# Where the activation tiles lie in SBUF: each at another multiple of 64 bytes past a 512-byte boundary, the weight tiles on the boundary as before

## The chip, the cores and the metric

One Trainium2 chip, one of its cores. The metric is the device time of one execution in microseconds (us); the kernel is run several times and the median is compared. All tensors are float32; most matmuls read their operands as float32r (`F32R` in the code).

## The reference, cut to what matters

One layer of a hybrid encoder on 256 tokens with a model width of 2048: an input projection to attention and to a gated recurrence (HGRN2), both mixed and projected, a squared-ReLU MLP of width 8192, a per-layer embedding with a gate, and a final RMSNorm. Nearly all of its arithmetic is in the products of the 256 x 2048 activations with weight matrices:

```python
proj = jnp.einsum('bsd,de->bse', rmsnorm(x, g_mix[i]), w_in[i])
...
y_attn = jnp.einsum('bse,ed->bsd', bidirectional_gqa(q_a, k_a, v_a), w_o_attn[i])
y_hgrn = jnp.einsum('bse,ed->bsd', o_r, w_o_hgrn[i])
mixed = jax.nn.sigmoid(gate_a) * y_attn + jax.nn.sigmoid(gate_r) * y_hgrn
x = x + jnp.einsum('bsd,de->bse', mixed, w_out[i])
u = jnp.square(jax.nn.relu(jnp.einsum('bsd,df->bsf', rmsnorm(x, g_mlp[i]), w_up[i])))
x = x + jnp.einsum('bsf,fd->bsd', u, w_down[i])
ple_gate = jax.nn.sigmoid(jnp.einsum('bsd,de->bse', rmsnorm(x, g_ple[i]), w_ple_gate[i]))
x = x + ple_gate * jnp.einsum('bsc,cd->bsd', p[i].astype(x.dtype), w_ple[i])
return rmsnorm(x, g_final)
```

## The kernel before

Every operand of a large product is split in two float32r parts, `hi` (a rounded copy) and `lo` (the rest), and three of the four partial products are summed: hi x hi, hi x lo and lo x hi.

Weights stream from HBM one 1 MB tile at a time, in the order of a list made beforehand (`order`, `plan`). `load` brings a tile into `raw` (three buffers), `prep_half` lets ScalarE copy half of it to a `hi` tile (L112) and VectorE subtract to get the `lo` tile (L113). `hi` and `lo` have four buffers of 4096 bytes per partition each.

Activations stand in tiles of 16384 bytes per partition, shaped [128, 8, 2, 256]: eight blocks of 128 features, for each the hi and the lo part, for each 256 tokens. Two such tiles make the 2048 features. They come from `bigt`, which takes the next of six buffers of one pool (`big`), and in two later stages from pools on the right-hand side of SBUF (`MX0`, `MX1`; `UB0`, `UB1`). `bigt` also gives the buffers of x, the residual rows and the final gain.

There are two forms of product:

- `gemm_mov` (L196): the stationary operand, which TensorE loads ahead of a matmul, is a 128x128 piece of an activation tile; the moving operand, which streams through, is 512 columns of a weight tile. All projections but two stages use it, w_ple's product (L699) has the same form. 5,232 matmuls in all.
- `gemm_st` (L177 and L178): the stationary operand is a piece of a weight tile; the moving operand is a block of an activation tile. L177 streams hi and lo of the activations together (512 columns) past the hi weights, L178 streams hi alone (256 columns) past the lo weights, and the two alternate. 1,792 such pairs: 768 in the recurrence's inputs (between some 229 and 713 us), 1,024 in the MLP's up-projection.

The recurrence (`scan_head`) and attention (`attend`) are generators, and small pieces of their work are put between the large matmuls; their tiles (`QQ`, `KK`, `kc`, `SD` and others; `qT`, `kT`, `pt`, `va`) come from right-hand pools too. PE runs its instructions in the order of the program; every matmul has a weight load of its own, which is issued when the matmul ahead of it starts.

A tile's byte address within a partition follows from the order and sizes of the pools. A tile without further use (`pad`, or the unnamed `ctile([P, 104])`) moves what stands behind it. What the address leaves when it is divided by 512 is called the offset here. In the kernel before, these are the offsets of what TensorE reads:

| Tiles | read at | offset before |
|---|---|---|
| weights `hi`, `lo` | L177, L178, L196 | 0 |
| activations `big`, `MX`, `UB` | L177, L178, L196 | 0 |
| `kT` moving, `qT` stationary | L424 | 352, 224 |
| `pt` moving, `va` stationary | L444 | 224, 224 |
| `QQ`, `kc`, `KK`, `SD` | L510, L536, L544 | 448 |

Pieces inside such tiles start at whole multiples of 512 bytes, so these are the offsets of every read.

Of the kernel before, what the change touches and what calls it, by code (L numbers as in the profile page):

```python
# [4 lines left out]
F32 = mybir.dt.float32  # L5
# [7 lines left out]
P = 128  # L13
# [13 lines left out]
def build(tc, xT, xtok, pT, gains, gfin_in, ropet, ident_in, masks_in, ghg_in, lb_in,  # L27
# [4 lines left out]
    def view(t, off, dims):  # L32
        return bass.AP(t.tensor, t.offset + off, [list(t.ap[0])] + [list(d) for d in dims])
# [35 lines left out]
    with contextlib.ExitStack() as es:  # L69
        def open_pool(name, bufs=1, **kw):  # L70
            st = contextlib.ExitStack()
            p = st.enter_context(tc.tile_pool(name=name, bufs=bufs, **kw))
            return p, st
# [4 lines left out]
        big, st_ = open_pool("big", 6); es.enter_context(st_)  # L78
# [5 lines left out]
        def nm(s):  # L84
            cnt[0] += 1
            return f"{s}_{cnt[0]}"

        def bigt(dt, shape):
            return big.tile(shape, dt, tag="big", name=nm("big"))

        def gps():
            return psg.tile([P, 512], F32, tag="g", name=nm("g"))
# [46 lines left out]
        def weave(gen):  # L139
            woven.append([gen, 0.0])  # L140
# [14 lines left out]
        def flush():  # L155
            while woven:
                advance(min(woven, key=lambda en: en[1]))
# [8 lines left out]
        def xs(X, k):  # L166
            return X[k // 8][:, k % 8]

        def gemm_st(key, X, last=None):

            his, los = next_w(key)
            ps = gps()
            for k in range(KT):
                if k == 12 and last:
                    last()
                x = xs(X, k)
                pe.matmul(ps, wsl(his, k, P), x, start=k == 0, stop=False)  # L177
                pe.matmul(ps[:, :S], wsl(los, k, P), x[:, 0, :], start=False, stop=k == KT - 1)  # L178
                tick(0.327)
            return ps  # L180

        def merge(ps, z):
            act.activation(z, ps[:, S:], AF.Copy)
            dve.tensor_tensor(z, ps[:, :S], z, ALU.add)
            return z

        def gemm_mov(arr, j, X, last=None, stagger=False):

            ps = [gps() for _ in range(NT)]

            def chunk(c, w, ts):
                for a, ws in ((0, w[0]), (1, w[0]), (0, w[1])):
                    for kk in range(4):
                        k = 4 * c + kk
                        for t in ts:
                            last_mm[0] = pe.matmul(ps[t], xs(X, k)[:, a, t * P:(t + 1) * P], wsl(ws, kk, 512),  # L196
                                                   start=k == 0 and a == 0 and ws is w[0],
                                                   stop=k == KT - 1 and ws is w[1])
                        tick(0.216 * len(ts))

            for c in range(2 if stagger else 4):
                if c == 3 and last:
                    last()
                chunk(c, next_w((arr, j, c)), range(NT))
            if stagger:
                if last:
                    last()
                ws = [next_w((arr, j, c)) for c in (2, 3)]
                for t in range(NT):
                    for c in (2, 3):  # L210
                        chunk(c, ws[c - 2], (t,))
            return ps

        def proj(g, X):
            return gemm_mov("in", GROUPS.index(g), X)

        def to_T(srcs, X, e0, gain=None):

            yield 2.5
            for e in (e0, e0 + 2):  # L220
                tp = mps()
                for a in range(2):
                    for t in range(NT):
                        o = (e - e0 + a) * P
                        pe.transpose(tp[:, a * S + t * P:a * S + (t + 1) * P], srcs[t][:, o:o + P], ident)  # L225
                if gain is None:
                    dst = X[e // 8][:, e % 8:e % 8 + 2]
                    tv = tp.rearrange("p (e t) -> p e t", e=2)
                    act.activation(dst[:, :, 0, :], tv, AF.Copy)
                    dve.tensor_tensor(dst[:, :, 1, :], tv, dst[:, :, 0, :], ALU.subtract)  # L230
                else:
                    for a in range(2):
                        dst, tv, g = xs(X, e + a), tp[:, a * S:(a + 1) * S], gain[:, e + a:e + a + 1]
                        act.activation(dst[:, 0, :], tv, AF.Copy, scale=g)
                        dve.scalar_tensor_tensor(dst[:, 1, :], tv, g, dst[:, 0, :], ALU.mult, ALU.subtract)  # L235
                yield 0.5
# [18 lines left out]
        rp = t1([P, 2, 2 * NT, HD], "qT")  # L255
        mkf = t1([P, len(LEVELS), P], "pt")
        xf = bigt(F32, [P, KT, S])
        xg = bigt(F32, [P, KT, S])
        Hx = [bigt(F32R, [P, 8, 2, S]) for _ in range(2)]
        Hm = []  # L260
        quarter = lambda X, qd: X[qd // 2][:, 4 * (qd % 2):4 * (qd % 2) + 4]
# [332 lines left out]
        for j in range(4):  # L594
            ya, yb = ctok("ya"), ctok("yb")
            ps = proj(f"a{j}", Hm)
            for t in range(NT):
                act.activation(ya[t], ps[t], AF.Sigmoid)
            ps = gemm_mov("oa", j, OA)
            for t in range(NT):  # L600
                dve.tensor_tensor(ya[t], ps[t], ya[t], ALU.mult)
            ps = proj(f"b{j}", Hm)
            for t in range(NT):
                act.activation(yb[t], ps[t], AF.Sigmoid)
            if j == 0:
                flush()
                st2.close()
                ph3, st3 = open_pool("ph3", side="right")
                MX = [ph3.tile([P, 8, 2, S], F32R, tag=f"MX{i}", name=nm("MX")) for i in range(2)]
                ph3.tile([P, 120], F32, tag="pad", name=nm("pad"))  # L610
            ps = gemm_mov("oh", j, OH)
            for t in range(NT):
                dve.tensor_tensor(yb[t], ps[t], yb[t], ALU.mult)
                dve.tensor_tensor(ya[t], ya[t], yb[t], ALU.add)
            weave(to_T(ya, MX, 4 * j))
# [10 lines left out]
        def squares(i, j, t):  # L626
            act.activation(junk(), rows(j)[t], AF.Square, accum_out=sums[i][:, t, j:j + 1])

        def row_r(i, ts=slice(0, NT)):

            r = rr[i][:, ts]
            dve.tensor_reduce(r, sums[i][:, ts], AX.X, ALU.add)
            dve.tensor_scalar(r, r, 1.0 / D, EPS, ALU.mult, ALU.add)  # L633
            rsq(r, r, ts.stop - ts.start)
# [12 lines left out]
        for step in MLP:  # L647
            c = int(step[1])
            if step[0] == "u":
                for f in range(16):  # L650
                    ps = gemm_st(("up", c * 16 + f), H1, last=flush if c == f == 0 else None)
                    if c == f == 0:
                        st3.close()
                        ph4, st4 = open_pool("ph4", side="right")

                        def t4(shape, tag, bufs=2, dt=F32):
                            return ph4.tile(shape, dt, tag=tag, bufs=bufs, name=nm(tag))

                        row_r(0)
                        dve.tensor_tensor(r1s, rr[0], rr[0], ALU.mult)  # L660
                        UA = [bigt(F32R, [P, 8, 2, S]) for _ in range(2)]
                        UB = [t4([P, 8, 2, S], f"UB{i}", 1, F32R) for i in range(2)]
                        t4([P, 120], "pad", 1)
                    r = merge(ps, t4([P, S], "r"))
                    uu = t4([P, S], "uu")
                    dve.scalar_tensor_tensor(uu, r, 0.0, r, ALU.max, ALU.mult)
                    u = xs(UA if c % 2 == 0 else UB, f)
                    act.activation(u[:, 0, :], uu, AF.Copy)
                    dve.tensor_tensor(u[:, 1, :], uu, u[:, 0, :], ALU.subtract)
                continue  # L670
            if c == 3:
                Hp = [bigt(F32R, [P, 8, 2, S]) for _ in range(2)]
            for j in range(4):
                ps = gemm_mov("dn", 4 * c + j, UA if c % 2 == 0 else UB)
                for t in range(NT):
                    xj = rows(j)[t]
                    dve.scalar_tensor_tensor(xj, ps[t], r1s[:, t:t + 1], xj, ALU.mult, ALU.add)
                    if c == 3:
                        squares(1, j, t)
                if c == 3:  # L680
                    weave(to_T(rows(j), Hp, 4 * j, gn[:, 2]))
# [137 lines left out]
```

## Time and profile before

| | |
|---|---|
| median of 3 runs | 1988.33 us (1988.01 to 1990.47) |
| profiled execution, its own time | 1988.49 us |
| its span, first to last instruction | 1986.7 us |
| mean granted TensorE clock | 0.997 of full speed |
| PE busy | 1960.8 us, 99% of the span |
| DVE, ACT busy | 62%, 48% |
| mean DMA rate | 180 GB/s |

The span is what the trace covers; the execution's own time is 1.8 us longer. PE is TensorE's matmuls, PEld its weight loads, DVE is VectorE, ACT is ScalarE. A matmul's end is modelled in this profile: it stands some 160 ns after the start of the next one, so the pace of a stream is read from starts, and the "mean ns of one" of two matmul groups differ by as much as their paces do.

### The profile page before, as it was taken

Reading aid. Unit: us, or ns where it says so; the run is one execution under the profiler, and the core shown is the slowest. Engines: PE = TensorE matmul, PEld = TensorE weight load, DVE = VectorE, ACT = ScalarE, POOL = GpSimd, SP = SyncE. Lnnn points to the kernel's source line nnn. Section 1 sums busy time; section 2 is a strip of 40 time slices with the busy share of each in tenths; the row PEclk is TensorE's granted clock in tenths of the full one; section 3 lists DMA queues with packets and bytes.
Section 4 is the critical chain, followed back from the end, with each engine's and each line's share of the span. In section 5 each row is a group of like instructions: output and inputs, shape, how many; then the busy total and the mean of one; then the engine's idle time right before and its main releaser. Section 6 shows DMA issues by size and latency. Waiting matters only on the chain.

```text
span 1986.7 us, 25647 instructions
## 1 busy us (share of the span) xinstructions
PE 1960.8 (99%) x9948; PEld 1661.6 (84%) x9948; DVE 1237.5 (62%) x1722; ACT 947.6 (48%) x1495; POOL 144.9 (7%) x175
## 2 busy tenths in 40 slices
PE   8999999999999999999999999999999999999998
PEld 6788888888888888888888888888888888888886
DVE  6877687686785884445545566665565456545555
ACT  5576555454554554434434454443344344434543
POOL 3300030120220210000000000000000000000001
PEclk9999999999999999999999999999999999999999
DMA  8444444544434445555565555555555555555553
GB/s 324 168 146 149 149 149 148 173 146 162 165 140 170 159 141 189 190 191 191 190 234 196 191 173 188 191 190 192 191 188 191 194 185 181 199 196 177 208 194 123
DMA packets 51673, 358.56 MB, mean 180 GB/s; under 512 B 5984, under 2 KB 6240, under 8 KB 9056
## 3 DMA queue, kind: packets, MB, share of 16 engines
q1 hardware_dynamic: 51552, 356.93, 50.7%
q8 instruction: 78, 1.28, 0.2%
q14 instruction: 43, 0.35, 0.0%
HBM read 354.81 MB, written 2.10 MB: 180 GB/s over the span
## 4 chain that ended last, share of the span: by engine, by line
PE 96%; DVE 2%; issue 1%; ACT 1%; DMA 0%; SPq 0%; POOLq 0%; POOL 0%; DVEq 0%; ACTq 0%
PE g L196 58%; PE g L177 20%; PE g L178 10%; PE m L510 3%; DVE lo L113 1%; PE m L444 1%; PE m L424 1%; PE g L699 1%; PE m L225 1%; PE m L545 0%; PE m L530 0%; PE m L544 0%; PE m L455 0%; ACT hi L112 0%; PE m L396 0%
## 5 line engine op out<-in xcount | busy, mean ns | idle before, releaser
L113 DVE TENSOR_TENSOR lo<-raw,hi 128x1024 fp32r<-128x1024 f32 x660 | 811.7, 1248 | 645.2 <-ACT hi L112 589.5
L112 ACT ACTIVATE hi<-raw 128x1024 fp32r<-128x1024 f32 x660 | 679.0, 1055 | 801.1 <-PE g L196 457.7
L196 PE MATMUL g<-hi,big 128*128 128x512 f32 x2688 | 657.8, 393 | 9.6 <-ACT hi L112 9.6
L177 PE MATMUL g<-big,hi 128*128 128x512 f32 x1792 | 645.4, 403 | 0.0
L196 PEld LDWEIGHTS g<-hi,big 128*128 128x128 f32 x2688 | 500.8, 189 | 111.5 <-ACT hi L112 10.7
L178 PE MATMUL g<-big,lo 128*128 128x256 f32 x1792 | 502.6, 281 | 0.0
L177 PEld LDWEIGHTS g<-big,hi 128*128 128x128 f32 x1792 | 337.2, 188 | 78.6 <-DVE big L235 0.2
L196 PE MATMUL g<-lo,big 128*128 128x512 f32 x1344 | 343.8, 393 | 0.0
L178 PEld LDWEIGHTS g<-big,lo 128*128 128x128 f32 x1792 | 339.2, 189 | 0.4
L196 PEld LDWEIGHTS g<-lo,big 128*128 128x128 f32 x1344 | 249.1, 188 | 49.3 <-DVE lo L113 0.2
L196 PE MATMUL g<-hi,UB 128*128 128x512 f32 x512 | 122.1, 390 | 0.0
L196 PEld LDWEIGHTS g<-hi,UB 128*128 128x128 f32 x512 | 95.8, 188 | 19.7
L301 POOL TENSOR_TENSOR c<-c,c 128x2 f32<-128x2 f32 (+1 forms) x5 | 3.2, 640 | 1159.9 <-DVE c L633 1145.8
L510 PE MATMUL m<-QQ,kc 128*128 128x128 f32 x448 | 72.7, 285 | 3.1 <-ACT kc L502 2.7
L510 PEld LDWEIGHTS m<-QQ,kc 128*128 128x128 f32 x448 | 63.8, 190 | 11.6 <-ACT kc L502 5.6
L502 ACT ACTIVATE kc<-KK 128x256 f32<-128x256 f32 x112 | 47.8, 437 | 50.9 <-PE m L510 26.0
L524 POOL TENSOR_TENSOR T<-T 128x256 f32<-128x256 f32 (+2 forms) x96 | 54.0, 563 | 202.3 <-DVE T L588 186.5
L196 PE MATMUL g<-lo,UB 128*128 128x512 f32 x256 | 64.1, 391 | 0.0
L196 PE MATMUL g<-hi,MX 128*128 128x512 f32 x256 | 61.7, 391 | 0.0
L517 DVE TENSOR_TENSOR QQ<-QQ,T 128x256 f32<-128x256 f32 x112 | 52.1, 465 | 12.8 <-PE m L510 12.3
L514 DVE TENSOR_TENSOR KK<-KK,T 128x256 f32<-128x256 f32 x112 | 54.7, 491 | 5.5 <-ACT kc L502 2.6
L196 PEld LDWEIGHTS g<-lo,UB 128*128 128x128 f32 x256 | 47.8, 188 | 9.8
(145 smaller groups left out, 1099.3 us busy)
## 6 DMA issues: line engine op xcount, KB each, us to landing
raw<-w_mov SPq DMA_DIRECT2D x87, 1024.0 KB, 4.8
raw<-w_up SPq DMA_DIRECT2D x64, 1024.0 KB, 4.8
raw<-w_dn SPq DMA_DIRECT2D x64, 1024.0 KB, 4.8
raw<-w_st SPq DMA_DIRECT2D x48, 1024.0 KB, 4.8
raw<-w_oa SPq DMA_DIRECT2D x16, 1024.0 KB, 4.8
raw<-w_oh SPq DMA_DIRECT2D x16, 1024.0 KB, 4.8
raw<-w_out SPq DMA_DIRECT2D x16, 1024.0 KB, 4.8
raw<-w_pg SPq DMA_DIRECT2D x16, 1024.0 KB, 4.8
```

Source lines behind the costliest of these rows:

```text
L112: act.activation(hi, sl, AF.Copy)
L113: dve.tensor_tensor(lo, sl, hi, ALU.subtract)
L177: pe.matmul(ps, wsl(his, k, P), x, start=k == 0, stop=False)
L178: pe.matmul(ps[:, :S], wsl(los, k, P), x[:, 0, :], start=False, stop=k == KT - 1)
L196: last_mm[0] = pe.matmul(ps[t], xs(X, k)[:, a, t * P:(t + 1) * P], wsl(ws, kk, 512), start=k == 0 and a == 0 and ws is w[0], stop=k == KT ...
L225: pe.transpose(tp[:, a * S + t * P:a * S + (t + 1) * P], srcs[t][:, o:o + P], ident)
L424: pe.matmul(sc[:, t * S:(t + 1) * S], qT[:, i, a, t * P:(t + 1) * P], kT[:, j, b], start=n == 0, stop=n == 2)
L502: act.activation(kc.rearrange("p (n a b) -> p n a b", a=2, b=L), merged(KK, 0, L, S // (2 * L)), AF.Copy)
L510: pe.matmul(pl[:, t * P:(t + 1) * P], kc[:, t * P:(t + 1) * P], merged(QQ, t * P, L, P // (2 * L)), start=True, stop=True)
L514: dve.tensor_tensor(kv, kv, view(T, 1, [[2, nb // 2], [nb - 1, 2], [0, L]]), ALU.mult)
L517: dve.tensor_tensor(qv, qv, view(T, nb + 1, [[2, nb // 2], [-(nb + 1), 2], [0, L]]), ALU.mult)
L524: pool.tensor_tensor(Tn, view(T, 0, [[nb, 2], [2, nb // 2]]), view(T, 1, [[nb, 2], [2, nb // 2]]), ALU.mult)
```

## The change

`bigt` now takes 4096 + 16 elements (16448 bytes) instead of 16384 bytes for every buffer and returns a view of the wanted shape at its start. So the six buffers lie at offsets 0, 64, 128, 192, 256 and 320 instead of all at 0. Two pads grow, which moves `MX0` and `MX1` to offset 384 and `UB0` and `UB1` to 448. The weight tiles stay at 0, and the tiles of attention and of the recurrence stay where they were. No instruction is added, dropped or reordered: on each engine the list of instructions is the same, row for row.

```diff
         def bigt(dt, shape):
-            return big.tile(shape, dt, tag="big", name=nm("big"))
+            t = big.tile([P, 4096 + 16], dt, tag="big", name=nm("big"))
+            dims, n = [], 1
+            for d in reversed(shape[1:]):
+                dims.insert(0, [n, d])
+                n *= d
+            return view(t, 0, dims)
...
                 MX = [ph3.tile([P, 8, 2, S], F32R, tag=f"MX{i}", name=nm("MX")) for i in range(2)]
-                ph3.tile([P, 120], F32, tag="pad", name=nm("pad"))
+                ph3.tile([P, 152], F32, tag="pad", name=nm("pad"))
...
                         UB = [t4([P, 8, 2, S], f"UB{i}", 1, F32R) for i in range(2)]
-                        t4([P, 120], "pad", 1)
+                        t4([P, 136], "pad", 1)
```

How many matmuls read an activation tile at which offset after the change, counted in the program:

| offset of the activations | 0 | 64 | 128 | 192 | 256 | 320 | 384 | 448 |
|---|---|---|---|---|---|---|---|---|
| L196 and L699, stationary (5,232) | 1,200 | 768 | 192 | 672 | 864 | 384 | 384 | 768 |
| L177/L178 pairs, moving (1,792) | 384 | 896 | | | | 512 | | |

So 4,032 matmuls of the first form and 1,408 pairs of the second have their two operands at different offsets after the change; before, all have both at 0.

## Rows read from the trace of the kernel before

**Rows 1.** The page, engines: busy us, share of the span, instructions.

```profile
PE 1960.8 (99%) x9948; PEld 1661.6 (84%) x9948; DVE 1237.5 (62%) x1722; ACT 947.6 (48%) x1495; POOL 144.9 (7%) x175
```

**Rows 2.** The page, granted TensorE clock in 40 slices, tenths.

```profile
PEclk9999999999999999999999999999999999999999
```

**Rows 3.** The page, chain that ended last: shares by engine, by line.

```profile
PE 96%; DVE 2%; issue 1%; ACT 1%; DMA 0%; SPq 0%; POOLq 0%; POOL 0%; DVEq 0%; ACTq 0%
PE g L196 58%; PE g L177 20%; PE g L178 10%; PE m L510 3%; DVE lo L113 1%; PE m L444 1%; PE m L424 1%; PE g L699 1%; PE m L225 1%; PE m L545 0%; PE m L530 0%; PE m L544 0%; PE m L455 0%; ACT hi L112 0%; PE m L396 0%
```

**Rows 4.** The waits of PE: total us, times, longest.

```profile
PE g L196 <- ACT hi L112: 9.6, 2, 7.7
PE m L396 <- DVE za L389: 3.5, 1, 3.5
PE m L510 <- ACT kc L502: 2.7, 4, 0.7
```

**Rows 5.** The chain, longest pieces: start us, us, what, number of matmuls.

```profile
814.36 86.17 PE g L196 x380
...
1346.08 87.06 PE g L196 x384
1523.59 87.06 PE g L196 x384
1701.09 112.00 PE g L196 x494
```

**Rows 6.** The chain in 1180 to 1346 us, its longest pieces.

```profile
1180.01 0.24 PE g L177
1181.07 0.24 PE g L177
1182.13 0.24 PE g L177
1183.19 0.24 PE g L177
1236.19 0.24 PE g L177
```

**Rows 7.** Groups by shape, 640.80 to 641.55: three neighbouring L177 matmuls.

```profile
L177 PE MATMUL g<-big,hi 128*128 128x512 f32 x1 | 0.4, 403 | 0.0
...
L177 PE MATMUL g<-big,hi 128*128 128x512 f32 x1 | 0.4, 398 | 0.0
...
L177 PE MATMUL g<-big,hi 128*128 128x512 f32 x1 | 0.4, 395 | 0.0
```

**Rows 8.** Timeline of PE, two changes from L196: start us, us, instruction.

```profile
320.72 0.39 PE L196 MATMUL g<-hi,big 128*128 128x512 f32 x1
320.95 0.38 PE L536 MATMUL m<-QQ,KK 128*128 128x128 f32 x2
...
113.36 0.40 PE L196 MATMUL g<-hi,big 128*128 128x512 f32 x1
113.60 0.40 PE L444 MATMUL m<-pt,va 128*128 128x256 f32 x2
```

**Rows 9.** Groups by shape: first and last L196 before an L536 or L544.

```profile
L196 PE MATMUL g<-hi,big 128*128 128x512 f32 x1 | 0.4, 389 | 0.0
...
L196 PE MATMUL g<-hi,big 128*128 128x512 f32 x1 | 0.4, 388 | 0.0
```

**Rows 10.** Groups by shape: an L196 before an L424, one before an L444.

```profile
L196 PE MATMUL g<-hi,big 128*128 128x512 f32 x1 | 0.4, 396 | 0.0
...
L196 PE MATMUL g<-lo,big 128*128 128x512 f32 x1 | 0.4, 396 | 0.0
```

**Rows 11.** Timeline of PE, a change from L196 to L510.

```profile
310.67 0.63 PE L196 MATMUL g<-hi,big 128*128 128x512 f32 x2
311.13 0.38 PE L510 MATMUL m<-QQ,kc 128*128 128x128 f32 x2
```

**Rows 12.** Groups by shape, whole span: matmuls of 256 columns.

```profile
L178 PE MATMUL g<-big,lo 128*128 128x256 f32 x1792 | 502.6, 281 | 0.0
...
L444 PE MATMUL m<-pt,va 128*128 128x256 f32 x96 | 15.2, 288 | 0.0
L424 PE MATMUL m<-kT,qT 128*128 128x256 f32 x96 | 14.2, 283 | 0.0
```

**Rows 13.** Busy us of each engine by stretch, clock, DMA share, GB/s.

```profile
1200.00:1500.00 300.00, 300.00 (x1592) 256.83 (x1591) 177.03 (x229) 133.74 (x184) 0.00 (x0) 1.00 0.53 187
1500.00:1800.00 300.00, 300.00 (x1467) 252.90 (x1466) 164.32 (x190) 123.91 (x151) 0.00 (x0) 1.00 0.54 192
```

**Rows 14.** The page, DMA issues: KB each, median us to landing.

```profile
out_x<-big SPq DMA_DIRECT2D x8, 256.0 KB, 2.7
```

## The prediction

> **What bounds the kernel now.** I read the page's engine table first: PE is busy for 99% of the span, DVE for 62% and ACT for 48% [rows 1]. The clock line shows full speed in every slice [rows 2], so PE is not held by its clock. The chain that ended last is PE for 96%, and 88% of the span lies on three lines, L196, L177 and L178 [rows 3]. PE waits for almost nothing: its longest sum is 9.6 us, at the start, for the first weights [rows 4]. In the stretches from 1200 to 1800 us PE has no idle time at all while DVE is busy for 55 to 59%, ACT for 41 to 45% and the DMA engines for 53 to 54% [rows 13]. So a nanosecond less for each matmul shortens the span by as much, and the others have room to follow; one more lengthens it likewise. The question is only whether the place of an operand changes the pace of a matmul.
>
> Two paces matter. L196 runs in unbroken chains: 384 matmuls in 87.06 us, or 226.7 ns each, and the same 226.7 to 226.8 in the other three long pieces, which read different activation tiles [rows 5]. L177 and L178 alternate; the chain's longest pieces start exactly 1.06 us apart, and three pairs fit in each 1.06 us, so a pair takes 353.3 ns. From 1183.19 to 1236.19 there are 50 such periods without a slip [rows 6]. Within a period the three L177 differ by up to 8 ns (403, 398 and 395 as the profile models their ends) [rows 7], although all their addresses are at offset 0.
>
> How much of this could go? Between a matmul of 512 columns, 389 ns [rows 9], and the three groups of 256 columns, 281 to 288 ns [rows 12], lie 101 to 108 ns: 0.39 to 0.42 ns a column, which is one cycle of the upper clock level, 2.4 GHz (0.417 ns). 512 columns at that rate are 213.3 ns, so L196 carries 13.4 ns beyond its columns. A pair has 768 columns, 320.0 ns, and carries 33.3 ns.
>
> **The change part by part.** It removes, adds and moves no instruction; each engine's list is the same. What changes is where PE reads and where ACT, DVE and some DMAs read and write.
>
> *The stationary operand at another offset (L196, L699).* 4,032 of 5,232 matmuls load their activation piece from an offset of 64 to 448 while 512 columns of a weight tile at offset 0 stream. The trace of before holds this case in small: where an L196 is followed by a matmul of the recurrence, the load that runs beside it comes from offset 448 [rows 8]. Of the 16 such places before an L536 or L544 the first shows 389 ns and the last 388 [rows 9], the figure of an undisturbed L196 at offset 0. Where the next matmul is one of attention's, the load comes from offset 224, and L196 takes 396 ns [rows 10], 7 to 8 more. 448 is a multiple of 64 and 224 is not; the change uses only multiples of 64. So the bounds are 0 and 7.5 ns for each of 4,032 matmuls, 0 to +30.2 us. A gain is not excluded either, since 13.4 ns of each are unexplained (−54.0 us). I take 0, because 448 is nearest in kind to the new offsets, and one of them. A blemish: before some L510, at 448 too, the pace is slower (two matmuls from 310.67 to 311.13, 0.46 us) [rows 11]; those follow a disturbed matmul, so I count it as disturbance.
>
> On this the Trainium skill (SBUF — State Buffer, section "Who interferes with whom") says that TensorE has independent read ports for the moving operand and for the weight load, and that it waits for no other engine. By that rule no offset would matter and the sum would be nil; the trace agrees at 448 but not at 224, where the measured 7 to 8 ns decide. By the row at 224, taken for all, the time would be 2018.5 us.
>
> *The moving operand at another offset (L177, L178).* 1,408 of 1,792 pairs stream activations from offset 64 or 320 past weights loaded from 0. No row shows a stream of 512 float32r columns from an offset other than 0. The nearest are those of 256 columns: L178, both at 0, 281 ns; L424, moving at 352 and stationary at 224, 283; L444, both at 224, 288 [rows 12]. The two that differ in offset lie between those that don't, so the difference of offsets leaves no mark here. Bounds: the same 7.5 ns for each of 2,816 matmuls, +21.1 us; all of the 33.3 ns returned, −46.9 us. I take 0.
>
> *ACT, DVE and DMA on the moved tiles.* They write the same numbers of elements. Should some of their instructions become a few ns longer, the 41% to 59% of idle time in [rows 13] hides it, since PE never waited for them there. Where that cover is gone, behind the last matmul, the eight output DMAs of 256 KB read moved rows at a median of 2.7 us [rows 14]; 5% on the last would be 0.14 us. Taken as 0.
>
> The sum: 0 + 0 + 0. The profiled execution took 1988.49 us (a span of 1986.7 and 1.8 around it), the median of the runs is 1988.33; the forecast is 1988.3 us.
>
> **The rivals.**
>
> *Collision, faster (chance 0.20).* The part beyond the columns may be a collision of the stream with the load beside it, both starting at offset 0 a few ns apart, and different offsets would part them. For it: L196 and L177 stream the same 512 columns at paces 6 to 14 ns apart [rows 7, 9], and the three L177 of a period differ at equal offsets, so something about timing matters. Against it: the load from 448 gained nothing [rows 9]. If all of it went where offsets now differ: 4,032 x 13.4 + 1,408 x 33.3 ns = 54.0 + 46.9 us, which gives 1887.4 us; half of it gives 1937.9.
>
> Beside this stands a rule of the Trainium skill (TensorE: Matmul & The Clock Gate, "Back-to-back issue gap"): a matmul in a warm stream is said to take its columns at 2.4 GHz plus about 2.5 ns. By it, as an estimate, 215.8 ns for L196 and 325.0 for a pair were possible, and their return where offsets differ would make 1904.5 us. The trace does not agree with the rule here, at 226.7 and 353.3 ns, and does not say why.
>
> *A place off 512 costs, slower (chance 0.14).* What cost 7 to 8 ns at offset 224 might be not the odd 32 bytes but the crossing of some larger boundary that 448 happens to spare and 64 to 384 do not. Then L196 alone gives +30.2 us, 2018.5 us; with the moving side too, 2039.6. It decides as soon as the mean pace of L196 is over 1 ns up (4,032 x 1 ns is the 0.2% below). Against it: 448 is itself no multiple of 128 or 256, and showed no cost.
>
> *Another rhythm of the pairs (0.09 each way).* The period of three in [rows 6, 7] is a balance between load and stream. A stream from another offset may settle at the quickest of its steps or the slowest: L177 at 395 or 403 in place of the mean of 398.7. With 1,408 pairs that is −5.2 us (1983.1) or +6.1 us (1994.4).
>
> *The place does not matter (0.48)*, as long as it is a multiple of 64: the forecast.
>
> **How the numbers follow.** About 0.2% (4 us) is what a measurement of this kernel can tell from no change; the likeliest case by itself is 1984.4 to 1992.3 us. It takes a mean shift under 0.7 ns over the 4,032 + 1,408 sites, so it is a narrow case, and I give it no more than 0.48. Faster: 0.20 + 0.09 = 0.29. Slower: 0.14 + 0.09 = 0.23. The range goes to the middle of the collision's case below (1938) and to the price of L196 alone above (2019); this leaves out about half of either rival, 0.17.
>
> **What would show it.** In the chain after: the piece of 384 L196 near 1523 us reads `UB` at 448, that near 1346 us reads tiles at 0 and 256. If I am right, all stay at 226.7 ns. A pace near 214 to 220 would show the collision; one near 234 would show that place costs; a difference between the two pieces would show which offset does what. Around 1180 to 1346 us the pairs read offsets 320 and 64 in turn, eight each; three pairs in 1.06 us would show that the moving side doesn't care, another period the new rhythm. The 1,200 matmuls still at offset 0 should keep 226.7 whatever happens. A shift of DVE or ACT means a time of one instruction on `big`, without effect on the span. I would be wrong, above all, if offsets other than 448 behave unlike 448, or if a stream of 512 columns minds its offset where one of 256 does not.

## The result and the profile after

The changed kernel takes 2000.32 us (median of 4 runs) against 1988.17 us: a ratio of 1.0062, 95% interval 1.0044 to 1.0079. It is slower by some 12 us. The forecast of no change was wrong; the time lies inside the range, on the side that I gave 0.23.

The page of the changed kernel, its engines (busy us, share of the span, instructions):

```profile
PE 1972.4 (99%) x9948; PEld 1663.8 (83%) x9948; DVE 1237.8 (62%) x1722; ACT 947.5 (47%) x1495; POOL 144.6 (7%) x175
```

Against [rows 1] PE is busy 11.6 us longer, DVE and ACT are as they were, and the count of instructions is the same. The waits of PE in the changed kernel (total us, times, longest) show that nothing new is waited for:

```profile
PE g L201 <- ACT hi L117: 10.4, 3, 7.5
PE m L401 <- DVE za L394: 3.4, 1, 3.4
PE m L515 <- ACT kc L507: 2.6, 4, 0.7
```

So the 12 us are in the pace of the matmuls. Line numbers have moved by five: L196 of before is L201, L177 and L178 are L182 and L183. Some of the longest pieces of the chain in the changed kernel (start us, us, what, number of matmuls):

```profile
1109.47 21.38 PE g L201 x92
...
1355.87 87.05 PE g L201 x384
1532.24 87.89 PE g L201 x384
...
1900.11 83.39 PE g L201 x360
```

The piece at 1355.87 reads tiles at offsets 0 and 256: 87.05 / 384 = 226.7 ns, the pace of before [rows 5]. That at 1532.24 reads `UB` at 448: 228.9 ns. That at 1109.47 reads `MX` at 384: 232.4 ns. The last reads tiles at 192 and 320: 231.6 ns. Some places cost up to 6 ns per matmul, one costs nothing, and none gains. Three quarters of the pairs in the up-projection keep their period of 1.06 us, as the same view of the changed kernel in 1270 to 1300 us shows first. The third quarter, from 1443 to 1532 us, reads the same tiles and goes quicker, as the view in 1440 to 1532 us shows behind it:

```profile
1270.01 0.24 PE g L182
1271.07 0.24 PE g L182
1272.13 0.24 PE g L182
1273.19 0.24 PE g L182
...
1445.02 0.24 PE g L182
...
1448.16 0.24 PE g L182
...
1451.30 0.24 PE g L182
```

There the period is 3.14 us for nine pairs, 348.9 ns a pair. Summed over the trace, from start to start, the 5,033 steps between neighbouring L196 (L201 here) take 14.5 us more than before and the 1,683 steps from pair to pair take 1.9 us less.

That raised two theories. **A, the distance**: what counts is how far the place that TensorE loads from lies from the place that it streams from, counted within 256 bytes (0 and 256 alike, 64 and 320 alike, 128 and 384 alike). **B, the load's own place**: a load that doesn't start on a multiple of 256 costs, wherever the stream is. A third, that the growth came from the buffers being 64 bytes larger or unlike each other, had to be excluded. "Distance" is, from here, the load's offset less the stream's, modulo 256.

### The profile page after: what moved, and what is told of

It is laid out like the page before. It is cut to its first block, busy times and chain, and to the rows that moved or that the text cites. A ratio compares the mean times of both kernels' runs of the same rounds, so it can differ in the third digit from the quotient of the medians.

```text
span 1999.0 us, 25647 instructions
## 1 busy us (share of the span) xinstructions
PE 1972.4 (99%) x9948; PEld 1663.8 (83%) x9948; DVE 1237.8 (62%) x1722; ACT 947.5 (47%) x1495; POOL 144.6 (7%) x175
## 4 chain that ended last, share of the span: by engine, by line
PE 95%; DVE 3%; issue 1%; ACT 1%; POOL 0%; DMA 0%; SPq 0%; POOLq 0%; DVEq 0%; ACTq 0%
PE g L201 57%; PE g L182 20%; PE g L183 10%; PE m L515 3%; DVE lo L118 1%; PE m L449 1%; PE m L429 1%; PE g L704 1%; PE m L230 1%; PE m L550 0%; PE m L535 0%; PE m L549 0%; PE m L460 0%; DMA big<-xT 0%; DVE big L274 0%
## 5 line engine op out<-in xcount | busy, mean ns | idle before, releaser
L201 PE MATMUL g<-hi,big 128*128 128x512 f32 x2688 | 664.7, 395 | 10.4 <-ACT hi L117 10.4
L182 PE MATMUL g<-big,hi 128*128 128x512 f32 x1792 | 643.3, 400 | 0.0
L201 PEld LDWEIGHTS g<-hi,big 128*128 128x128 f32 x2688 | 501.6, 189 | 118.3 <-ACT hi L117 11.7
L183 PE MATMUL g<-big,lo 128*128 128x256 f32 x1792 | 503.3, 281 | 0.0
L182 PEld LDWEIGHTS g<-big,hi 128*128 128x128 f32 x1792 | 337.2, 188 | 75.6 <-DVE big L240 0.2
L201 PE MATMUL g<-lo,big 128*128 128x512 f32 x1344 | 346.9, 395 | 0.0
L183 PEld LDWEIGHTS g<-big,lo 128*128 128x128 f32 x1792 | 337.1, 188 | 0.4
L201 PEld LDWEIGHTS g<-lo,big 128*128 128x128 f32 x1344 | 249.3, 189 | 51.9
L201 PE MATMUL g<-hi,UB 128*128 128x512 f32 x512 | 123.1, 392 | 0.0
L201 PEld LDWEIGHTS g<-hi,UB 128*128 128x128 f32 x512 | 95.9, 188 | 20.7
L515 PEld LDWEIGHTS m<-QQ,kc 128*128 128x128 f32 x448 | 64.0, 190 | 11.6 <-ACT kc L507 5.4
L201 PE MATMUL g<-lo,UB 128*128 128x512 f32 x256 | 64.6, 393 | 0.0
L201 PE MATMUL g<-hi,MX 128*128 128x512 f32 x256 | 63.1, 396 | 0.0
L201 PEld LDWEIGHTS g<-hi,MX 128*128 128x128 f32 x256 | 47.9, 188 | 10.9
```

The costliest lines, as they stand in the source:

```text
L515: pe.matmul(pl[:, t * P:(t + 1) * P], kc[:, t * P:(t + 1) * P], merged(QQ, t * P, L, P // (2 * L)), start=True, stop=True)
```

## The experiments

All keep the instructions and their order, and change addresses only, except the two with half loads. Each ratio is against runs of the kernel before on the same chip.

**All activations at 64.** A pad ahead of the six buffers of `bigt`, as it was before, and other pads behind `MX` and `UB`:

```diff
+        big.tile([P, 16], F32, tag="pad", bufs=1, name=nm("pad"))
...
-                ph3.tile([P, 120], F32, tag="pad", name=nm("pad"))
+                ph3.tile([P, 104], F32, tag="pad", name=nm("pad"))
...
-                        t4([P, 120], "pad", 1)
+                        t4([P, 104], "pad", 1)
```

> All activation tiles at offset 64, weights at 0, so each of the 5,232 matmuls of L196 and L699 has the pair of offsets that showed about 5.5 ns more in the changed kernel (0 and 64). If the place of the operands sets the pace (either by the load's own place or by its distance from the stream's): 5,232 x 5.5 ns = +29 us, the L177/L178 pairs as in the changed kernel (about -0.5 ns each, -1 us), so some 2016 us, 1.4% above before. If the added time of the changed kernel came instead from the six buffers having different offsets (their 64 bytes more each, not the place itself): no change, 1988 us.

Measured: 2016.11 us, ratio 1.0142 (1.0125 to 1.0159). The long pieces of its chain:

```profile
820.28 88.67 PE g L198 x380
...
1361.64 89.60 PE g L198 x384
1540.56 89.61 PE g L198 x384
```

89.60 / 384 is 233.3 ns, 6.6 more than before, in all stages alike. The place sets the pace; unlike buffers are not needed.

**All activations at 256**, the same edit with pads of 64, 56 and 56 elements.

> All activation tiles at offset 256, weights at 0. If the pace goes by the place within 256 bytes: 1988 us, L196 at 226.7 ns as with offset 0. If it goes by the place within 512 bytes (and the tiles at 256 in the changed kernel kept their pace by chance): between 0 and +29 us. If any place other than the weights' costs: about +12 us or more.

Measured: 1988.09 us against 1988.31, ratio 1.0000 (0.9991 to 1.0010). 256 is as good as 0.

**Weights and activations at 64.** The pad ahead of all big pools grows, and those behind `MX` and `UB` shrink, so that every large operand is at 64:

```diff
-        ctile([P, 104])
+        ctile([P, 120])
...
-                ph3.tile([P, 120], F32, tag="pad", name=nm("pad"))
+                ph3.tile([P, 104], F32, tag="pad", name=nm("pad"))
...
-                        t4([P, 120], "pad", 1)
+                        t4([P, 104], "pad", 1)
```

> Weights and activations both at offset 64, so that their distance is 0 again. Theory A, the distance between stream and load sets the pace: 1988 us, L196 at 226.7 ns, pairs at 353 ns. Theory B, the load's own place past a boundary of 256 bytes sets it: L196 +5.5 ns x 5,232 = +29 us, and the loads of the pairs (3,584 weight pieces, now at 64) up to as much each, +20 us: 2017 to 2037 us.

Measured: 1987.04 us against 1988.31, ratio 0.9995 (0.9985 to 1.0004). The chain of this kernel:

```profile
816.39 86.16 PE g L196 x380
...
1344.71 87.05 PE g L196 x384
1522.20 87.06 PE g L196 x384
```

Every load of the large products is 64 bytes past a multiple of 256 here, and the pace is 226.7 ns again. Theory B falls: by it 29 us or more were due. The same loads that cost 6.6 ns with the stream at 0 cost nothing with the stream at 64.

Two more things stand in this trace. The tiles of the recurrence stayed at 448, so the loads of its float32 matmuls are now 128 bytes from the stream, modulo 256, where they were 192 from it in the kernel before. At all 16 places of [rows 9] the L196 in front of an L536 or L544 now takes 396 ns as the profile models its end, 7 to 8 more than there. One of them, from the groups by shape in 323.02 to 323.04 us:

```profile
L196 PE MATMUL g<-hi,big 128*128 128x512 f32 x1 | 0.4, 396 | 0.0
```

And the pairs, which were expected at 353 ns, have two paces at one distance. The chain in 1180 to 1340 us, then in 1460 to 1500 us:

```profile
1181.78 0.23 PE g L177
1183.86 0.23 PE g L177
...
1460.01 0.24 PE g L177
1461.07 0.24 PE g L177
```

In the first half of the up-projection six pairs take 2.08 us, 346.7 ns a pair; in the second half three take 1.06 us, 353.3 ns, with both operands at the same offsets.

**Only the weights at 64**, activations at 0: a pad of 16 elements between `raw` and `hi`, and one of 112 behind them that puts the later pools back.

> Only the split weight tiles at offset 64, activations at 0. Theory B (the load's own place): L196 loads activations at 0 and keeps 226.7 ns; the pairs load weights at 64, up to 5.5 ns more per load, 3,584 x 5.5 = +20 us, so 1988 to 2008 us, with all of the growth in L177 and L178. Theory A (the distance): L196 has its load 64 bytes behind the stream, the distance of the tiles at 448 in the changed kernel, which showed 229 ns: 5,232 x 2 ns = +10 us, in L196; pairs unknown.

Measured: 1999.23 us, ratio 1.0055 (1.0040 to 1.0070), 10.9 us more. L196 has the load 64 bytes behind the stream, distance 192, and its pieces of 384 take 87.90 us, 228.9 ns each, 2.2 more than before; the pairs keep their 353 ns. Theory B expected the growth in the pairs and none in L196. It is the other way round.

**All activations at 128, and at 192.** The first edit with other pads.

> All activations at offset 128, weights at 0: a distance of 128 between the load and the stream. The changed kernel's matmuls at 128 and 384 showed about 5 ns more: 5,232 x 5 = +26 us, some 2013 us, if the distance within 256 bytes sets the pace. If only distances of 64 past a multiple of 256 cost: 1988 us.

> All activations at offset 192, weights at 0. By the distance theory this is the case of the weights at 64 and the activations at 0 (the load 64 bytes behind the stream, within 256), and of offset 448: L196 at about 229.8 ns on the mean, +2.2 ns x 5,232 = +11 us, some 1999 us. If 448 was free because it is 448 and not because it is 192 past 256: another pace, up to +29 us.

Measured: 2012.28 us, ratio 1.0132 (1.0117 to 1.0147), and 1997.60 us, ratio 1.0057 (1.0040 to 1.0074). Both as expected. 192 agrees with the weights at 64 (1.0055), though other tiles were moved: the two have only their distance in common.

**All activations at 32.**

> All activations at offset 32, weights at 0: a distance that is no multiple of 64, as with the 224 in the kernel before (7.5 ns more). If the distance alone sets the pace, 32 lies between 0 (nothing) and 64 (+5.9 ns): 0 to +31 us. If an odd 32 bytes cost by themselves: 5,232 x 7.5 = +39 us in L196 and more in the pairs, 2027 us or over.

Measured: 2007.51 us, ratio 1.0106 (1.0091 to 1.0121). Less than an odd 32 bytes should have cost by themselves. L196 is slow, but the pairs are quick in the whole of the up-projection, and not in half of it as in the run with all at 64. The chain of this kernel in 1200 to 1350 us:

```profile
1200.89 0.23 PE g L179
1201.93 0.23 PE g L179
1202.97 0.23 PE g L179
1204.01 0.23 PE g L179
```

Three pairs take 1.04 us, 346.7 ns a pair, and L196 89.59 us for 384 or 233.3 ns.

**Sixteen distances in one run.** Each weight tile gets 64 elements of slack and starts at 16 bytes times its number modulo 16:

```diff
-            hi = wraw.tile([P, 1024], F32R, tag="hi", bufs=4, name=nm("hi"))
-            lo = wraw.tile([P, 1024], F32R, tag="lo", bufs=4, name=nm("lo"))
+            off = 4 * (i % 16)
+            hi, lo = (view(wraw.tile([P, 1088], F32R, tag=n, bufs=4, name=nm(n)), off, [[1, 1024]]) for n in ("hi", "lo"))
```

> Activations all at 0; each weight tile lies at 16 x (its number in the stream mod 16) bytes past a multiple of 256, so one run has 16 distances. If the distance sets the pace, the chunks at 64, 128 and 192 past show for L196 about 229.8, 233 and 233.4 ns (the load 64 behind, 128 and 64 ahead), the pairs with the load 224 past (32 behind) about 347 ns and those with 0 353. If the place of the activations were what counted, all chunks would show 226.7 and 353 ns. The steps of 16 bytes show whether some distance is better than 0 for L196, which none of the runs so far holds.

Measured: 2006.46 us, one run. Some starts in its timeline of PE (start us, us, instruction; a weight tile's 24 matmuls are 16 with `hi` and 8 with `lo`):

```profile
1383.36 3.91 PE L196 MATMUL g<-hi,big 128*128 128x512 f32 x16
...
1388.99 3.88 PE L196 MATMUL g<-hi,big 128*128 128x512 f32 x16
...
1394.58 3.80 PE L196 MATMUL g<-hi,big 128*128 128x512 f32 x16
...
1400.03 3.83 PE L196 MATMUL g<-hi,big 128*128 128x512 f32 x16
...
1405.51 3.87 PE L196 MATMUL g<-hi,big 128*128 128x512 f32 x16
...
1422.26 3.83 PE L196 MATMUL g<-hi,big 128*128 128x512 f32 x16
...
1427.77 3.85 PE L196 MATMUL g<-hi,big 128*128 128x512 f32 x16
```

The tile at 1383.36 has distance 48: (1388.99 − 1383.36) / 24 = 234.6 ns. Distance 16 starts at 1394.58: 227.1. Distance 0 at 1400.03: 228.3. Distance 192 at 1422.26: 229.6. The medians of the steps between starts, over some 300 steps for each distance of L196 and some 100 pairs:

| distance | 0 | 16 | 32 | 48 | 64 | 80 | 96 | 112 | 128 | 144 | 160 | 176 | 192 | 208 | 224 | 240 |
|---|---|---|---|---|---|---|---|---|---|---|---|---|---|---|---|---|
| L196, ns | 227 | 227 | 232 | 235 | 233 | 235 | 234 | 233 | 232 | 231 | 232 | 230 | 229 | 232 | 234 | 232 |
| pair, ns | 349 | 347 | 347 | 347 | 353 | 350 | 347 | 353 | 353 | 349 | 351 | 353 | 353 | 349 | 347 | 353 |

For L196 no distance beats 0; 16 is equal. For the pairs 224 is among the best. That the pairs at 0 would show 353 ns was wrong: the median is 349, and in the up-projection alone their mean is 346.5 ns at 0 and 346.9 at 224. The steps of one distance vary (at 240 those of L196 are 226 to 235 ns, with a mean of 231.5), so these medians are rough by 1 or 2 ns.

**Two distances, each where it is best.** The same edit, with the place chosen by the stage:

```diff
+            off = 56 if order[i][0] in ("st", "up") else 0
```

> Activations all at 0 as before; the weight tiles of the L177/L178 stages at 224 past a multiple of 256, those of the L196 stages at 0. The distance theory then has L196 as before (226.7 ns) and the pairs as in the run with the activations at 32 (346.8 instead of 352.8 ns): 1,792 x 6 = 10.8 us less than before, 1977 us. If the quicker pairs came from the activations' own place at 32: no change for the pairs, 1988 us.

Measured: 1979.36 us against 1988.73, ratio 0.9956 (0.9942 to 0.9969). This version beats both kernels, by 9.4 us against before; I had expected 10.8. The chain of this kernel, first in 1180 to 1346 us, then over the span:

```profile
1180.75 0.23 PE g L177
1181.79 0.23 PE g L177
1182.83 0.23 PE g L177
...
1338.83 87.05 PE g L196 x384
1514.64 87.05 PE g L196 x384
```

The pairs take 346.7 ns with all activations at 0, so it was not the activations' place at 32 that made them quick, and L196 keeps 226.7. Over the trace the 1,683 steps from pair to pair take 9.6 us less than before, which is about the gain. Distance 224 gave 346.7 ns throughout the up-projection in both runs that had it; distance 0 gave it in parts of others only, and what decides there is not shown.

**Half loads.** All matmuls of L196 but the first and last of each sum load 64 columns:

```diff
+                            m = P if (k == 0 and a == 0 and ws is w[0]) or (k == KT - 1 and ws is w[1]) else P // 2
-                            last_mm[0] = pe.matmul(ps[t], xs(X, k)[:, a, t * P:(t + 1) * P], wsl(ws, kk, 512),
+                            last_mm[0] = pe.matmul(ps[t][:m], xs(X, k)[:, a, t * P:t * P + m], wsl(ws, kk, 512),
```

> Offsets as before (all 0), but all matmuls of L196 except the first and the last of each sum load only 64 of their 128 stationary columns, which leaves out half of the output rows' sums. If the 13.4 ns that an L196 takes beyond its 512 columns are owed to the load beside it, about half go: 220 ns, some 5,100 x 6.7 = 34 us less, 1954 us. If they are a fixed cost of each matmul: 226.7 ns and 1988 us.

Measured: 1998.93 us, one run, with the two pieces of 384 at 88.33 us each, 230.0 ns. Neither expectation holds: with half the load the stream is slower, not quicker and not the same. Half of the output rows are left out, so this kernel is good for the pace alone. The pairs, in which nothing was changed, take 346.7 ns here in the second half of the up-projection and 353.3 in the first.

> The half loads of the run before it (64 of 128 stationary columns, the first and last matmul of each sum excepted, which leaves out half of the output rows' sums), now with the activations at offset 64. With full loads a distance of 64 raised an L196 from 226.7 to 233.3 ns, 6.6 more. If the cost of the distance is paid along the load, half of it should remain: 230.0 (the pace of half loads at distance 0) + 3.3 = 233 ns. If half loads no longer mind the distance: 230. If the cost is one per load, however long: 236 to 237 ns.

Measured: 2014.05 us, one run on another chip; the pieces of 384 take 89.34 us, 232.7 ns. That is 2.6 ns over half loads at distance 0, where full loads showed 6.6: less than half of the price, near the 233 expected of a price paid along the load. It is one run at each distance, and the reference pace of 230.0 is itself unexplained, so I take it as a hint.

## Why the prediction was wrong

*What bounds the kernel* held. PE is the bound, and each nanosecond of pace came through: the prices of the uniform runs, per matmul of L196 and L699, are 27.8 us / 5,232 = 5.3 ns at 64, 26.4 / 5,232 = 5.1 at 128, 11.8 / 5,232 = 2.2 at 192 and 0 at 256 (pairs included). With the counts of the change, 1,152 at 64 or 320, 576 at 128 or 384, 1,440 at 192 or 448 and 864 at 256, they give 6.1 + 2.9 + 3.2 + 0 = 12.2 us. Measured were 12.2 us (2000.32 − 1988.17). These prices are of whole kernels, the pairs included, so the close fit says little of either form alone; the trace has 14.5 us more in L196 and 1.9 us less in the pairs.

*The stationary operand at another offset* is the step that failed: "I take 0, because 448 is nearest in kind to the new offsets, and one of them." The row was right and the inference from it was not. What counts is the distance within 256 bytes; 448 stands for distance 192, the cheapest of the new distances that cost anything, and I let that one place speak for 64 and 128, which cost more than twice as much. Even at 192 the price is not nil: 2.2 ns in the uniform run, where [rows 9] showed none. Those rows are single steps behind a stream at distance 0, and a single step is not a pace: with all activations at 192 the steps of L196 come in turn at 229, 231 or 232 and 226 ns, so that some of them show no price at all. Three neighbours of that run, by shape, in 1400.57 to 1400.61, 1400.80 to 1400.84 and 1401.03 to 1401.07 us:

```profile
L198 PE MATMUL g<-lo,big 128*128 128x512 f32 x1 | 0.4, 392 | 0.0
...
L198 PE MATMUL g<-lo,big 128*128 128x512 f32 x1 | 0.4, 394 | 0.0
...
L198 PE MATMUL g<-hi,big 128*128 128x512 f32 x1 | 0.4, 388 | 0.0
```

That the loads in [rows 9] belong to float32 matmuls of 128 columns does not free them from the price: at distance 128, in the run with all at 64, they cost as much as others. The 7 to 8 ns of [rows 10] fit the price of distance 224 (234 ns against 227 in the scan). The slower step in [rows 11], also at 448, I put down to disturbance; it should have kept a bound of some nanoseconds in the likeliest case. The division into multiples of 64 and others was wrong too: 16 is free and 64 is not.

*The rule of the Trainium skill* (SBUF — State Buffer, "Who interferes with whom") is that TensorE's read ports for the moving operand and for the weight load are independent, and that it waits for no other engine. By that rule the distance would not matter, and the trace does not agree. With the same loads, streams and instructions, L196 takes 226.7 or 233.3 ns, by their distance alone. That the two reads get in each other's way somewhere is the plain reading, but no run shows the place.

*The moving operand* at nil was off by little: the pairs took 1.9 us less, with 348.9 ns in the third quarter of the up-projection and 353 in the rest. That it came near nil is in part luck, as the 346.7 ns at 224 show. The period of before was also not the only one at equal offsets, as the run with all at 64 shows.

*The rivals.* "A place off 512 costs" was the right sign and nearly the right size per matmul (5 to 7 ns where I had 7.5), with a wrong reason: it is the distance, and a multiple of 256 is as good as 512. "Collision, faster" had the right mechanism in that the load and the stream do interact, with the sign reversed for L196, where equal offsets are the best case. "Another rhythm of the pairs" did occur, in the third quarter of the changed kernel's up-projection for one, and it is what the best version lives on; its condition, a stream from another offset, was not needed, since the run with all at 64 had it at equal offsets. *ACT, DVE and DMA* at nothing held; their busy time did not change.

**What stays open.** Why the distance matters, and why within 256 bytes. Which of two paces the pairs take where both occur at the same offsets (at distance 0 in the run with all at 64, at 192 in the changed kernel and in the run with all activations at 64). The first run with half loads, which differs from the kernel before in L196 alone, suggests that the matmuls ahead of the pairs decide, but no run tested it. Where the rest of the 13.4 ns beyond the columns comes from, which every run of L196 keeps, and why half a load makes the stream slower. Whether other moving sizes or data types have the same distances was not tried, but for the float32 loads at 128 and 192.

## What to carry to other kernels

When PE is busy all the time, compare the pace of its matmuls with their columns, and look at the addresses: here the distance between where the load and the stream start, modulo 256 bytes, moved a matmul of 512 float32r columns between 226.7 and 233 ns, and equal offsets were the safe choice. Place the operands for each form of product by itself, since 224 was good for one and bad for the other; a scan that gives each tile another place finds candidates in one run, and a run with that one place throughout must confirm them. One row at one place does not bound the others, nor does a single step give the pace of a stream: a nil taken from it needs the range of the nearest rows that are not nil.

## What the runs showed of the hardware that I had not expected

The pace of an unbroken stream of L196 depends on the difference of two addresses and not on either: 226.7 ns with both operands at 0, with both at 64 and with 0 and 256, 233.3 ns with 0 and 64. The alternating pairs do not follow that order: 224 gave 346.7 ns throughout, although L196 at 224 is among the slow ones (234 ns). Nor does the distance settle their pace alone: at distance 0 they took 353.3 ns in the kernel before, and 346.7 and 353.3 ns in two stretches of one run. And a load of half the columns made the stream beside it slower, 230.0 against 226.7 ns, in one run.
